# Queries turned in the score banks, key stacks in halves, and three convolution chunks dealt out in parts

## Chip, cores and metric

The kernel runs on one core of a Trainium2 chip. The metric is the device time of one execution in microseconds (us); lower is better. The core's engines run side by side, each working off its own instructions in order, and wait for each other through semaphores: PE (matrix products, results in PSUM banks), ACT (activations, copies), DVE (elementwise work, reductions), POOL (elementwise work in SBUF) and SP (which issues the DMAs).

## The reference

Two layers over 16 learned meta tokens and a sequence of 1024, 1024 features wide. Each layer has a sliding-window attention with 16 heads of 64 on 2 key heads, and an mLSTM with 4 heads:

```python
def hybrid_layer(x, ...):
    h = rms_norm(x, norm_g)
    z = h @ w_in
    aq, ak, av, ag, mq, mk, mv, mi, mf, mo, mgate = jnp.split(z, split_points(), axis=-1)
    q = apply_partial_rope(rms_norm(aq.reshape(B, L, 16, 64), q_norm_g), cos, sin)
    k = apply_partial_rope(rms_norm(ak.reshape(B, L, 2, 64), k_norm_g), cos, sin)
    ya = sliding_window_sink_attention(q, k, v, sink).reshape(B, L, ATT_WIDTH) * jax.nn.silu(ag)
    qk = jax.nn.silu(causal_depthwise_conv(jnp.concatenate([mq, mk], axis=-1), conv_w, conv_b))
    hm = mlstm_chunkwise(mq, mk, mv, log_i, log_f)          # mq, mk: the halves of qk
    ym = rms_norm(hm) * jax.nn.sigmoid(mo) * jax.nn.silu(mgate)
    return x + jnp.concatenate([ya, ym], axis=-1) @ w_out
```

## The kernel before

All matrix products are made of float32r pieces: an operand is split into a high part (a copy to float32r, mostly on ACT) and a low part (what is left, a subtraction on DVE or POOL), and three products are added up in PSUM. Such pairs of a high and a low part are called stacks below.

A layer (`l` is 0 for the first, 1 for the second) goes through keys and values, attention, mLSTM and the output projection. During attention PE has two streams of work, written out by hand and kept in that order (`pin`, `in_order`):

- The foreground list `fg`: projections, cut into parts of some 6 to 9 matmuls by `projT_parts` and `projN_parts`. A projection collects in one bank of the pool `pj`, which has two; when it is complete, `done` evacuates it. Even blocks `j` project the gates (`g_tasks`, evacuated at L640), odd ones the next queries (`q_tasks`), block 7 the mLSTM's values (`v_parts`).
- The background list: for each pair of heads `j` (8 of them) and each tile `b` of 128 queries (9 in the first layer, 8 in the second) four steps. `s1` makes the scores of two heads in a bank pair `S` (L667, alternating between two tiles `SS`) and the softmax from them: masks, a reduction (L685), two exponentials (L688), a reciprocal and two scalings (L693). `s2`, two steps later, transposes the probabilities into the bank `T` (L704, L707) and splits them (L711 to L715). `s3` and `s4`, another step later, multiply by the values in the bank `O` (L731, L743), which L746 and L748 evacuate. `T` and `O` have one bank each.

`weave` deals the background out between the foreground parts. Extra work hangs on foreground parts by number (`at`): among it `q_stacks(j, g)`, which takes a `pj` bank, transposes four tiles of rotated queries X into it (L617), and writes the query stack with two copies (L600, L601) and two subtractions (L602, L603) of 64x512. `g` is the half: tiles 1 to 4 or 5 to 8. X is complete after the rotation on DVE, whose last write is L556. In the first layer the 16 meta queries are turned in a corner of an `O` bank (`QM`), evacuated by the same L600 to L603 at 64x16.

Heads 8 to 15 need the second key head, so the key stacks `Ks` are rewritten between `j` = 3 and 4: `k_stacks(1, g, i)` four times, each a copy (L436) and a subtraction (L437) of 64x576. The scheduler may order everything that is not on PE, and does so by its own simulation.

At the end of attention the first three steps' worth of blocks are still to drain ("tail"); `cv` holds the six chunks (two projections by three ranges of tokens, 272, 384 and 384 wide) of the first mLSTM head's convolution (`conv_tasks`). Two of them stand between the draining steps as whole projections of 24 matmuls (L186), each followed by its copy, four multiply-adds, a tanh and a last product. Then the banks `S`, `T`, `O` are given up for others, `in_order` ends, and `gates` follows with the remaining chunks.

Of the kernel before, what the change touches and what calls it, by code (L numbers as in the profile page):

```python
# [14 lines left out]
AF = mybir.ActivationFunctionType  # L15
ALU = mybir.AluOpType
# [19 lines left out]
EARLY = 80  # L36
FIRST = ((0, 0), (0, 1), (1, 0))
# [26 lines left out]
def build(ctx, tc, I, O):  # L64
# [4 lines left out]
    def pin(ins):  # L69

        return tc.keep_in_program_order(ins) if in_order[0] else ins
# [293 lines left out]
    for l in range(DEPTH):  # L365
# [64 lines left out]
        def k_stacks(kv, g, i):  # L430

            s0 = 64 * kv
            src = KT[s0:s0 + 64, 4 * g:4 * g + 4].rearrange("p a c -> p (a c)")
            d = 64 - s0 if i else s0
            hi, lo = [T[d:d + 64, 576 * g:576 * g + 576] for T in Ks]
            sc.activation(hi, src, AF.Copy)  # L436
            ve.tensor_tensor(lo, src, Ks[0][s0:s0 + 64, 576 * g:576 * g + 576], op=ALU.subtract)  # L437
# [181 lines left out]

        def q_meta_turn(j, ps):  # L620
            c0 = 128 * (j % 2)
            pin(pe.transpose(ps, A[j]["q"]["XM"][:, c0:c0 + 128], ident[:16, :16]))
# [30 lines left out]
        def att_tasks(j, st):  # L653
# [3 lines left out]
            def s1(b):  # L657
                t0, p = TT[b]
                S = SS[blk[0] % 2]
                blk[0] += 1  # L660
                k0, kn, o = (0, 16, 128) if b == 0 else (0, 144, 128) if b == 1 else (16 + (b - 2) * 144, 272, 0)
                for h in range(2):
                    U = st["Q", b > 4]
                    i = (b - 1) % 4
                    lq = U[:, 1024 + 16 * h:1040 + 16 * h] if b == 0 else U[:, 512 * h + 128 * i:512 * h + 128 * i + 128]
                    for i in range(2):
                        pin(pe.matmul(S[:p, h, o + 2 - 2 * h:o + 2 - 2 * h + kn], lq, Ks[i][:, k0:k0 + kn],  # L667
                                  start=(i == 0), stop=(i == 1)))
                if st.setdefault("S", 0) < 2:
                    ve.tensor_copy(cols(S, 1, 783, 1), snk[:, l, 2 * j:2 * j + 2].rearrange("p (h c) -> p h c", c=1))  # L670
# [20 lines left out]
                for h in range(2):  # L691
                    Pn = P[:p, 1 + 144 * h:145 + 144 * h]
                    sc.activation(Pn, Pn, AF.Copy, scale=mx[:p, 2, h:h + 1])  # L693
                live[b] = P
# [154 lines left out]
        def conv_tasks(h, wgf, st):  # L849
            def chunk_task(which, c):  # L850
# [8 lines left out]
                ps = projT(wgf(), 128 * which, t0, n)  # L859
# [10 lines left out]
            return [lambda w=w, c=c: chunk_task(w, c) for w in range(2) for c in range(3)]  # L870
# [172 lines left out]
        for j in range(8):  # L1043
# [11 lines left out]
        at = {n0 + 6: [lambda: k_turn(0), lambda: (k_stacks(0, 0, 0), k_stacks(0, 0, 1)), lambda: v_stacks(0, 0)],  # L1055
              n0 + 15: [lambda: k_turn(1), lambda: (k_stacks(0, 1, 0), k_stacks(0, 1, 1)), lambda: v_stacks(0, 1)],
# [10 lines left out]
        ns = len(steps) // 8  # L1067

        def step(i):

            out = [lambda: None] * (2 * (i < 3) + (i < 2))
            if i < len(steps):
                j, b, s1 = steps[i][:3]
                out.append(lambda: s1(b))
                if (j, b) in ((3, 6), (3, 7), (4, 1), (4, 2)):
                    out.append(lambda: k_stacks(1, j - 3, b - 6 if j == 3 else b - 1))
# [12 lines left out]
        for j in range(8):  # L1089
# [16 lines left out]
            if j == 7:  # L1106
                at.setdefault(10, []).append(lambda: q_stacks(7, 1))
            else:
                at.setdefault((9 if j else 8) + extra, []).append(lambda j=j: q_stacks(j, 1))
                at.setdefault(21 + extra if j % 2 else 20, []).append(lambda j=j: q_stacks(j + 1, 0))  # L1110
# [8 lines left out]
        cv = conv_tasks(0, wc[0], M[0])  # L1119
        weave(cv[:2], step(8 * ns) + step(8 * ns + 1) + step(8 * ns + 2))  # L1120
# [3 lines left out]
        for f in cv[2:]:  # L1124
            f()
# [181 lines left out]
```

## Time and profile before

| | us |
|---|---|
| median of 3 runs | 1950.03 (1949.86 to 1952.85) |
| the profiled execution, its time | 1953.92 |
| its span, first to last instruction | 1952.2 |
| PE busy | 1908.1 (98%) |
| DVE, ACT, POOL busy | 1088.3, 1067.7, 906.4 |
| attention of the first layer | about 78 to 395 of the span, its tail to 412 |
| attention of the second layer | about 1068 to 1358, its tail to 1376 |

Rows of the profile name a line of the kernel, the engine, the operation, and the tiles it writes and reads. In rows in order of time the first number is the start in us from the span's start, the second how long it took; what stands in brackets is how long the engine idled before it and what ended that. In the list of waits stand the total, the number of waits and the longest.

### The profile page before, as it was taken

What the parts mean: (1) busy time and instruction counts of PE and PEld (TensorE: products, weight loads), DVE (VectorE), ACT (ScalarE), POOL (GpSimd) and SP (SyncE); (2) the same over time, 40 slices, a digit from 0 to 9 for tenths busy, and PEclk for the clock granted to TensorE, in tenths of its full rate; (3) what the DMA queues carried; (4) which work ended last, traced back from release to release, by engine and by line L of the source; (5) the groups of instructions that cost most, each with busy time, mean ns of one, the idle gap of its engine ahead of it and who ended that gap; (6) DMA issues with size and microseconds to landing.
All of it is one profiled execution on the core that took longest, in us unless ns stands there. A gap on an engine that the chain in (4) does not pass through costs nothing.

```text
span 1952.2 us, 36164 instructions
## 1 busy us (share of the span) xinstructions
PE 1908.1 (98%) x12827; PEld 1799.7 (92%) x12827; DVE 1088.3 (56%) x2966; ACT 1067.7 (55%) x3133; POOL 906.4 (46%) x1102
## 2 busy tenths in 40 slices
PE   8999999999999999999999999999999999999999
PEld 7998898999999999977789999999999999998887
DVE  7777777667454363532445678776673635437211
ACT  6577776747454544643334777776464535446221
POOL 3544544336545454564325345444365444547332
PEclk9999999999999999999999999999999999999999
DMA  4111111121222121455541111112122121226543
GB/s 153 44 37 49 39 43 35 37 65 35 62 60 58 41 56 55 146 164 168 176 132 50 39 37 54 43 36 59 39 58 64 40 67 50 57 62 187 171 149 121
DMA packets 150838, 148.28 MB, mean 76 GB/s; under 512 B 15081, under 2 KB 123921, under 8 KB 150658
## 3 DMA queue, kind: packets, MB, share of 16 engines
q1 hardware_dynamic: 150658, 145.97, 25.5%
q8 instruction: 101, 1.65, 0.4%
q14 instruction: 79, 0.65, 0.1%
HBM read 122.58 MB, written 23.29 MB: 75 GB/s over the span
## 4 chain that ended last, share of the span: by engine, by line
PE 80%; DVE 6%; ACT 4%; issue 3%; POOL 3%; DMA 3%; SPq 0%; POOLq 0%; DVEq 0%; ACTq 0%
PE pj L186 35%; PE pj L226 13%; PE pss L1204 6%; PE pj L1204 6%; PE po L1204 5%; PE po L917 2%; PE S L667 2%; PE pss L917 2%; DMA raw<-in_w_in_dram 2%; PE O L743 2%; POOL RING L160 1%; PE O L731 1%; PE pt L917 1%; ACT t L688 1%; PE T L707 1%
## 5 line engine op out<-in xcount | busy, mean ns | idle before, releaser
L186 PE MATMUL pj<-H,RING 128*128 128x384 f32 (+2 forms) x3456 | 583.0, 322 | 0.0
L186 PEld LDWEIGHTS pj<-H,RING 128*128 128x128 f32 x3456 | 543.3, 188 | 2.5 <-issue 0.2
L160 POOL TENSOR_TENSOR RING<-raw,RING 128x512 fp32r<-128x512 f32 (+1 forms) x192 | 255.5, 1338 | 121.5 <-ACT RING L159 114.4
L226 PE MATMUL pj<-RING,H 128*128 128x256 f32 (+1 forms) x1920 | 268.3, 286 | 3.5 <-DVE u L640 3.5
L226 PEld LDWEIGHTS pj<-RING,H 128*128 128x128 f32 x1920 | 242.5, 189 | 4.0 <-DVE u L640 3.8
L226 PE MATMUL pj<-H,RING 128*128 128x384 f32 (+2 forms) x1152 | 215.0, 326 | 3.9 <-DVE u L603 3.9
L186 PE MATMUL pj<-RING,H 128*128 128x256 f32 x1536 | 209.9, 287 | 3.3 <-DVE H L300 1.6
L178 POOL TENSOR_TENSOR RING<-raw,RING 128x512 fp32r<-128x512 f32 x96 | 125.9, 1318 | 175.8 <-ACT RING L177 167.3
L186 PEld LDWEIGHTS pj<-RING,H 128*128 128x128 f32 x1536 | 193.8, 191 | 6.1 <-DVE H L300 2.1
L226 PEld LDWEIGHTS pj<-H,RING 128*128 128x128 f32 x1152 | 179.4, 189 | 4.8 <-PE T L707 2.3
L177 ACT ACTIVATE RING<-raw 128x512 fp32r<-128x512 f32 x128 | 80.7, 631 | 173.0 <-DMA raw<-in_w_out_dram 139.6
L159 ACT ACTIVATE RING<-raw 128x512 fp32r<-128x512 f32 (+1 forms) x196 | 122.8, 630 | 66.1 <-DMA raw<-in_w_in_dram 50.4
L752 POOL TENSOR_TENSOR u<-u,w1k 128x128 f32<-128x128 f32 (+1 forms) x136 | 63.7, 468 | 172.7 <-DVE w1k L748 168.6
L688 ACT ACTIVATE t<-S,mx 128x145 f32<-128x145 f32 (+1 forms) x272 | 100.3, 373 | 59.8 <-DVE mx L685 52.7
L718 POOL TENSOR_SCALAR_AFFINE_SELECT p<-p 128x512 fp32r<-128x512 f32 x112 | 72.4, 646 | 126.9 <-DVE p L714 126.4
L930 POOL TENSOR_TENSOR p<-u,p 128x258 fp32r<-128x258 f32 x64 | 49.7, 777 | 170.8 <-ACT p L929 155.6
L1204 PE MATMUL pss<-RING,H 128*128 128x512 f32 x384 | 120.5, 394 | 0.0
L1204 PE MATMUL pj<-RING,H 128*128 128x512 f32 x352 | 110.7, 396 | 0.0
L693 ACT ACTIVATE t<-t,mx 128x144 f32<-128x144 f32 (+1 forms) x272 | 97.5, 407 | 20.3 <-DVE mx L690 20.1
L866 DVE SCALAR_TENSOR_TENSOR t<-u,cw,t 128x384 f32<-128x384 f32 (+1 forms) x144 | 107.2, 744 | 2.2
L886 DVE SCALAR_TENSOR_TENSOR t<-t,pj 128x384 f32<-128x384 f32 (+2 forms) x48 | 24.5, 511 | 124.8 <-ACT t L885 124.7
L748 DVE TENSOR_TENSOR w1k<-O,w1k 64x128 f32<-64x128 f32 (+1 forms) x272 | 74.6, 274 | 34.2 <-ACT w1k L746 31.3
(344 smaller groups left out, 3804.6 us busy)
## 6 DMA issues: line engine op xcount, KB each, us to landing
raw<-in_w_out_dram SPq DMA_DIRECT2D x128, 256.0 KB, 2.8
raw<-in_w_in_dram SPq DMA_DIRECT2D x100, 256.0 KB, 2.8
raw<-in_w_in_dram SPq DMA_DIRECT2D x192, 128.0 KB, 2.3
spool<-u SPq DMA_DIRECT2D x56, 192.0 KB, 1.9
p<-x SPq DMA_DIRECT2D x24, 256.0 KB, 3.6
t<-spool SPq DMA_DIRECT2D x30, 192.0 KB, 3.4
p<-spool SPq DMA_DIRECT2D x26, 192.0 KB, 4.2
u<-em SPq DMA_DIRECT2D x8, 576.0 KB, 6.5
```

Source lines behind the costliest of these rows:

```text
L159: sc.activation(hi, raw[:, :, 0:o], AF.Copy)
L160: eng.tensor_tensor(lo, raw[:, :, 0:o], hi, op=ALU.subtract)
L177: sc.activation(hi, raw, AF.Copy)
L178: (ve if i > 8 and i % 2 else gp).tensor_tensor(lo, raw, hi, op=ALU.subtract)
L186: last = pin(pe.matmul(out, a, b, start=(i == 0), stop=(i == n - 1)))
L226: pin(pe.matmul(out(), x, y, start=(k + i == 0), stop=(k == n - 1 and i == 2)))
L688: sc.activation(P[:p, 145 * h:145 * h + 145], S[:p, h, 1 + 127 * h:146 + 127 * h], AF.Exp, bias=mx[:p, 0, h:h + 1], accum_out=mx[:p, 1, h: ...
L693: sc.activation(Pn, Pn, AF.Copy, scale=mx[:p, 2, h:h + 1])
L748: ve.tensor_tensor(y[64 * h:64 * h + 64, :p], O[0:64, p * h:p * h + p], up[0:64, p * h:p * h + p], op=ALU.add)
L866: ve.scalar_tensor_tensor(z, RAW[:, t0 + i:t0 + i + n], wcol(i), z, ALU.mult, ALU.add)
L917: pin(f(*a, **k))
L1204: pin(pe.matmul(ps[:p, :], a, b, start=(i + n == 0), stop=(i == 15 and n == len(terms) - 1)))
```

## The change

A query stack gets no bank of its own. The scores of a tile fill columns 1 to 274 or so of each of the two banks of `S`; `visits` gives each second step or so a visit: right behind the score matmuls of `s1`, `q_turn` transposes two query tiles into columns 384 to 511 of the two banks, and at the end of `s1` `q_take` writes them to the query stack, with two copies and two subtractions of 64x256. There are two visits for a former `q_stacks`, 30 in each layer, and each lies two steps ahead of the block that first needs it. The very first stack of a layer stays as it was.

`k_stacks` now takes a start and a number of tiles, and `KEYS` spreads the second key head over eight steps, two tiles each time.

`conv_tasks` can give its first chunks in parts, as the foreground lists do; the first three chunks are now 3, 4 and 4 parts, dealt out over the draining steps.

```diff
+KEYS = {(3, 6): (0, 2, 0), (3, 7): (0, 2, 1), (3, 8): (2, 2, 0), (4, 1): (2, 2, 1),
+        (4, 2): (4, 2, 0), (4, 3): (4, 2, 1), (4, 4): (6, 2, 0), (4, 5): (6, 2, 1)}
...
-        def k_stacks(kv, g, i):
+        def k_stacks(kv, a, n, i):
...
-            hi, lo = [T[d:d + 64, 576 * g:576 * g + 576] for T in Ks]
+            hi, lo = [T[d:d + 64, 144 * a:144 * a + 144 * n] for T in Ks]
...
+        def q_turn(S, j, g, i):
+
+            c0 = 128 * (j % 2)
+            X = A[j]["q"]["X", g == 1]
+            for k in range(2):
+                pin(pe.transpose(S[:, k, 384:512], X[:, 256 * (i + k) + c0:256 * (i + k) + c0 + 128], ident))
+
+        def q_take(S, j, g, i):
+
+            Q = q_unit(j, g)[:, 0:1024].rearrange("p (h a c) -> p h a c", h=2, a=4)[:, :, i:i + 2]
+            src = S[:, :, 384:512]
+            sc.activation(Q[0:64, 0], src[0:64], AF.Copy)
+            sc.activation(Q[64:128, 1], src[64:128], AF.Copy)
+            ve.tensor_tensor(Q[64:128, 0], src[0:64], Q[0:64, 0], op=ALU.subtract)
+            ve.tensor_tensor(Q[0:64, 1], src[64:128], Q[64:128, 1], op=ALU.subtract)
...
+                if visit:
+                    q_turn(S, *visit)
...
+                if visit:
+                    q_take(S, *visit)
...
+            every = [(w, c) for w in range(2) for c in range(3)]
+            first = [x for w, c in every[:parted]
+                     for x in projT_parts(wgf, 128 * w, *CH[c][:2], lambda ps, w=w, c=c: finish(w, c, ps))]
+            return first + [lambda w=w, c=c: whole(w, c) for w, c in every[parted:]]
...
+        visits = {j * ns + 4 * g + i + 1 - first_q - 2: (j, g, i)
+                  for j in range(8) for g in range(2) for i in (0, 2) if j + g > 0}
...
-                if (j, b) in ((3, 6), (3, 7), (4, 1), (4, 2)):
-                    out.append(lambda: k_stacks(1, j - 3, b - 6 if j == 3 else b - 1))
+                k = KEYS.get((j, b))
+                if k:
+                    out.append(lambda: k_stacks(1, *k))
...
-            if j == 7:
-                at.setdefault(10, []).append(lambda: q_stacks(7, 1))
-            else:
-                at.setdefault((9 if j else 8) + extra, []).append(lambda j=j: q_stacks(j, 1))
-                at.setdefault(21 + extra if j % 2 else 20, []).append(lambda j=j: q_stacks(j + 1, 0))
...
-        cv = conv_tasks(0, wc[0], M[0])
-        weave(cv[:2], step(8 * ns) + step(8 * ns + 1) + step(8 * ns + 2))
+        cv = conv_tasks(0, wc[0], M[0], 3)
+        nt = len(cv) - 3
+        weave(cv[:nt], step(8 * ns) + step(8 * ns + 1) + step(8 * ns + 2))
...
-        for f in cv[2:]:
+        for f in cv[nt:]:
             f()
```

What that does to the engines' orders is seen at three places. Rows name line, operation, output, inputs and shape; "x9" is nine alike in a row, and what a row waits for stands in brackets. Lines of the changed kernel are higher: L686 are the scores (before L667), L627 `q_turn`, L635 and L636 `q_take`, L439 the key subtraction, L727 and L730 the transposes into `T`, L754 and L766 the products into `O`, L228 projection parts.

PE in the second layer, `j` = 3, around the turn for the first half of `j` = 4. Before:

```order
L743 MATMUL O<-ptm_106,VM 128x128 x2
L743 MATMUL O<-p_15103,u 128x256 [waits Pool_49]
L743 MATMUL O<-p_15103,u 128x256
L617 MATMUL pj<-cst,u 128x128 x4
L226 MATMUL pj<-RING,H 128x256 x6
L667 MATMUL S_13188<-u 128x272 x4
L704 MATMUL T<-cst,t 32x128 [waits DVE_49,PE_49]
```

After:

```order
L686 MATMUL S_13240<-u 128x272 x4
L627 MATMUL S_13240<-cst,u 128x128 [waits DVE_49]
L627 MATMUL S_13240<-cst,u 128x128
L228 MATMUL pj<-RING,H 128x256 x6
L727 MATMUL T<-cst,t 32x128 [waits PE_49,Activation_49]
L730 MATMUL T<-cst,t 128x128 x2
```

Four transposes into `pj` became twice two behind a tile's scores, one step further ahead, and the first of these two waits for DVE.

DVE in the first layer, end of `j` = 3 and start of `j` = 4, between one block's evacuation of `O` and the next one's. Before:

```order
L748 TENSOR_TENSOR w1k<-O,w1k 64x128
L681 COPY_PREDICATED S_1046<-mask,S_1046 128x2x128 [waits PE_49]
L685 TENSOR_REDUCE mx<-S_1046 128x2 [waits DVE_49]
L602 TENSOR_TENSOR u<-pj,u 64x512 [waits Activation_49]
L603 TENSOR_TENSOR u<-pj,u 64x512
L437 TENSOR_TENSOR u<-u 64x576 [waits Activation_49]
L437 TENSOR_TENSOR u<-u 64x576
L690 RECIPROCAL mx<-mx 128x2 [waits Activation_49]
L670 COPY S_1045<-snk 128x2 [waits PE_49]
L714 TENSOR_TENSOR p_3308<-T,p_3308 128x256 [waits Activation_49]
L715 TENSOR_TENSOR ptm_106<-T,ptm_106 32x128
```

After:

```order
L771 TENSOR_TENSOR w1k<-O,w1k 64x128
L702 COPY_PREDICATED S_1046<-mask,S_1046 128x2x128 [waits PE_49]
L439 TENSOR_TENSOR u<-u 64x288 [waits Activation_49]
L439 TENSOR_TENSOR u<-u 64x288
L706 TENSOR_REDUCE mx<-S_1046 128x2 [waits DVE_49]
L711 RECIPROCAL mx<-mx 128x2 [waits Activation_49]
L737 TENSOR_TENSOR p_3328<-T,p_3328 128x256 [waits PE_49,Activation_49]
L738 TENSOR_TENSOR ptm_106<-T,ptm_106 32x128
L635 TENSOR_TENSOR u<-S_1046,u 64x256 [waits Activation_49]
L636 TENSOR_TENSOR u<-S_1046,u 64x256
L691 COPY S_1045<-snk 128x2 [waits PE_49]
```

The query's subtractions are half as wide and behind the split of `T`'s results (L737, L738) instead of ahead of it, and the key subtractions are half as wide.

PE in the first layer's tail. Before:

```order
L186 MATMUL pj<-H,RING 128x272 x24
L704 MATMUL T<-cst,t 32x128 [waits DVE_49,PE_49]
L707 MATMUL T<-cst,t 128x128 x2
L731 MATMUL O<-p_5660,u 128x256 [waits DVE_49,Activation_49]
L731 MATMUL O<-p_5660,u 128x256
L743 MATMUL O<-ptm_106,VM 128x128 x2
L743 MATMUL O<-p_5665,u 128x256 [waits Pool_49]
L743 MATMUL O<-p_5665,u 128x256
L704 MATMUL T<-cst,t 32x128 [waits DVE_49,PE_49]
L707 MATMUL T<-cst,t 128x128 x2
L186 MATMUL pj<-H,RING 128x384 x24
```

After:

```order
L730 MATMUL T<-cst,t 128x128 x2
L228 MATMUL pj<-H,RING 128x272 x9
L754 MATMUL O<-p_5713,u 128x256 [waits DVE_49,Activation_49]
L754 MATMUL O<-p_5713,u 128x256
L228 MATMUL pj<-H,RING 128x384 x12
L766 MATMUL O<-ptm_106,VM 128x128 x2
L766 MATMUL O<-p_5718,u 128x256 [waits Pool_49]
L766 MATMUL O<-p_5718,u 128x256
L228 MATMUL pj<-H,RING 128x384 x6
L727 MATMUL T<-cst,t 32x128 [waits DVE_49,PE_49]
L730 MATMUL T<-cst,t 128x128 x2
```

Projection parts of 9, 12 and 6 matmuls lie between two uses of `T`, where before there was none.

More of the change, by code (lines that the diff above doesn't have):

```diff
@@ L428, in k_turn @@
             sc.activation(KT[:, 4 * g:4 * g + 4, 16:144], ps[:, 0:512].rearrange("p (a c) -> p a c", a=4), AF.Copy)
-        def k_stacks(kv, g, i):
+        def k_stacks(kv, a, n, i):
             s0 = 64 * kv
-            src = KT[s0:s0 + 64, 4 * g:4 * g + 4].rearrange("p a c -> p (a c)")
+            src = KT[s0:s0 + 64, a:a + n].rearrange("p a c -> p (a c)")
             d = 64 - s0 if i else s0
-            hi, lo = [T[d:d + 64, 576 * g:576 * g + 576] for T in Ks]
+            hi, lo = [T[d:d + 64, 144 * a:144 * a + 144 * n] for T in Ks]
             sc.activation(hi, src, AF.Copy)
-            ve.tensor_tensor(lo, src, Ks[0][s0:s0 + 64, 576 * g:576 * g + 576], op=ALU.subtract)
+            ve.tensor_tensor(lo, src, Ks[0][s0:s0 + 64, 144 * a:144 * a + 144 * n], op=ALU.subtract)
         def v_stacks(kv, g):
@@ L659, in s1 @@
                 S = SS[blk[0] % 2]
+                visit = visits.get(blk[0])
                 blk[0] += 1
@@ L847, in v_parts, with conv_tasks, whole, finish @@
             return [x for t in range(9) for x in projN_parts(wgf, [t], 264, lambda ps, t=t: finish(t, ps))]
-        def conv_tasks(h, wgf, st):
-            def chunk_task(which, c):
+        def conv_tasks(h, wgf, st, parted=0):
+            def whole(which, c):
+                t0, n, _ = CH[c]
+                finish(which, c, projT(wgf(), 128 * which, t0, n))
+            def finish(which, c, ps):
                 tj = which * 4 + h
@@ L858, in chunk_task @@
                 t0, n, _ = CH[c]
-                ps = projT(wgf(), 128 * which, t0, n)
                 with tc.high_priority(offset=EARLY):
@@ L869, in chunk_task @@
                 ve.scalar_tensor_tensor(out[:, t0:t0 + n], th, 1.0, z, ALU.add, ALU.mult)
-            return [lambda w=w, c=c: chunk_task(w, c) for w in range(2) for c in range(3)]
+            every = [(w, c) for w in range(2) for c in range(3)]
+            first = [x for w, c in every[:parted]
+                     for x in projT_parts(wgf, 128 * w, *CH[c][:2], lambda ps, w=w, c=c: finish(w, c, ps))]
+            return first + [lambda w=w, c=c: whole(w, c) for w, c in every[parted:]]
         def mo_tasks(u, wgf, st, held=None):
@@ L1054, in build @@
         n0 = len(fq) - 24
-        at = {n0 + 6: [lambda: k_turn(0), lambda: (k_stacks(0, 0, 0), k_stacks(0, 0, 1)), lambda: v_stacks(0, 0)],
-              n0 + 15: [lambda: k_turn(1), lambda: (k_stacks(0, 1, 0), k_stacks(0, 1, 1)), lambda: v_stacks(0, 1)],
+        at = {n0 + 6: [lambda: k_turn(0), lambda: (k_stacks(0, 0, 4, 0), k_stacks(0, 0, 4, 1)), lambda: v_stacks(0, 0)],
+              n0 + 15: [lambda: k_turn(1), lambda: (k_stacks(0, 4, 4, 0), k_stacks(0, 4, 4, 1)), lambda: v_stacks(0, 1)],
               n0 + 21: [lambda: q_stacks(0, 0, "pss")] + ([lambda: q_meta(0, bank("po")[:, 0:16])] if first_q == 0 else [])}
```

## The prediction

> **What bounds the kernel.** I read the page's busy times first, then the chain that ended last, then the waits of PE, then busy time by stage.
>
> ```profile
> span 1952.2 us, 36164 instructions
> PE 1908.1 (98%) x12827; PEld 1799.7 (92%) x12827; DVE 1088.3 (56%) x2966; ACT 1067.7 (55%) x3133; POOL 906.4 (46%) x1102
> PE 80%; DVE 6%; ACT 4%; issue 3%; POOL 3%; DMA 3%; SPq 0%; POOLq 0%; DVEq 0%; ACTq 0%
> ```
>
> PE is the bound: 98% busy, and 80% of the chain. The change leaves PE's instruction count as it was (120 query transposes per pair of layers become the same 120 elsewhere), so all that it can win is idle PE time: 1952.2 - 1908.1 = 44.1 us. The stages tell where that lies (columns: stretch, length, busy us of PE, PEld, DVE, ACT, POOL, granted clock, DMA share, GB/s):
>
> ```profile
> 78.00:395.00 317.00, 301.21 (x2301) 292.21 (x2300) 228.90 (x686) 229.79 (x779) 137.66 (x191) 0.99 0.14 40
> 395.00:412.00 17.00, 15.77 (x110) 15.57 (x109) 10.96 (x29) 7.33 (x21) 7.46 (x11) 1.00 0.26 72
> 412.00:1068.00 656.00, 652.19 (x4100) 601.58 (x4099) 317.66 (x830) 310.63 (x833) 316.40 (x369) 1.00 0.31 91
> 1068.00:1358.00 290.00, 282.27 (x2186) 278.22 (x2185) 209.25 (x606) 210.04 (x690) 127.62 (x165) 1.00 0.16 43
> 1358.00:1376.00 18.00, 16.28 (x115) 16.08 (x114) 11.69 (x28) 7.62 (x23) 7.68 (x11) 1.00 0.26 70
> ```
>
> Attention of the first layer has 317 - 301.2 = 15.8 us of idle PE, of the second 7.7; the two tails, where the last blocks drain, 1.2 and 1.7. That is 26.4 us, the ceiling. The list of what PE waited for says which waits these are:
>
> ```profile
> PE O L731 <- DVE w1k L748: 6.4, 9, 1.7
> PE T L704 <- DVE ptm L715: 5.5, 5, 1.7
> PE pj L226 <- DVE u L603: 3.9, 5, 1.1
> PE pj L226 <- DVE u L640: 3.5, 3, 1.3
> PE O L731 <- DVE u L603: 2.8, 5, 1.1
> PE pj L617 <- DVE u L640: 2.2, 2, 2.0
> PE pj L210 <- DVE u L603: 0.5, 1, 0.5
> ```
>
> **Part one: queries no longer turned in a projection bank.** Each `q_stacks` took one of the two `pj` banks and gave it back after two copies and two subtractions, so the projection after next waited for L603. Those waits, 3.9 and 0.5, end, since no query uses `pj` any more: 4.4 us. The converse, the turning that waited for a bank (L617, 2.2), ends too, but 2.0 of it sits at the ramp of the second layer, and a `T` wait follows:
>
> ```profile
> 1077.27 0.66 PE L617 MATMUL pj<-cst,u 128*128 128x128 f32 x4 [1.96 <-DVE u L640]
> 1082.24 0.27 PE L704 MATMUL T<-cst,t 128*32 128x128 f32 x1 [1.37 <-DVE ptm L715]
> ```
>
> Without the first wait PE arrives at `T` earlier, while the softmax of that block is no earlier. Of these 3.3 us I take 2.0, between 0.6 and 3.3; with the other 0.2, this part gives 4.4 + 2.2 = 6.6. The `O` wait on L603 (2.8) is the meta query, which the change doesn't touch, and L640 (3.5) comes from two short projections in a row at a group's end: I cost both at nothing.
>
> The four evacuations become eight of half the width. Their price from the 512-wide and the 16-wide rows:
>
> ```profile
> L603 DVE TENSOR_TENSOR u<-pj,u x30: 693/693/694, 89.4 to 1339.1; 64x512 fp32r<-64x512 f32 x30
> L603 DVE TENSOR_TENSOR u<-O,u x7: 176/176/180, 104.8 to 349.6; 64x16 fp32r<-64x16 f32 x7
> L600 ACT ACTIVATE u<-pj x30: 570/592/594, 87.5 to 1337.2; 64x512 fp32r<-64x512 f32 x30
> L600 ACT ACTIVATE u<-O x7: 161/177/178, 104.2 to 349.0; 64x16 fp32r<-64x16 f32 x7
> ```
>
> DVE: (693 - 176) / 496 = 1.04 ns a column, 426 ns at 256; ACT 378. A stack costs DVE 4 x 426 - 2 x 693 = 318 ns more, ACT 328; for 30 stacks 9.5 and 9.8, 19.3 us in all, beside PE. Bounds: nothing where covered, 19.3 if never. PE idled for 23.5 of these 607 us, 4%, which is the share at which I charge it: -0.8.
>
> **Part two: key stacks in halves.** One place pays for bursts on DVE, the boundary of blocks 3 and 4 in the first layer:
>
> ```profile
> 231.89 0.68 DVE L602 TENSOR_TENSOR u<-pj,u 64x512 fp32r<-64x512 f32 x1 [0.28 <-ACT u L601]
> 232.59 0.69 DVE L603 TENSOR_TENSOR u<-pj,u 64x512 fp32r<-64x512 f32 x1
> 233.31 1.96 DVE L437 TENSOR_TENSOR u<-u 64x576 fp32r<-64x576 f32 x2
> 236.77 0.27 PE L704 MATMUL T<-cst,t 128*32 128x128 f32 x1 [0.88 <-DVE ptm L715]
> 238.95 0.57 PE L731 MATMUL O<-p,u 128*128 128x256 f32 x2 [1.69 <-DVE w1k L748]
> 230.00:240.00 10.00, 7.43 (x60) 6.99 (x59) 8.70 (x20) 9.79 (x28) 6.60 (x8) 0.96 0.20 53
> 240.00:250.00 10.00, 10.00 (x60) 9.64 (x60) 7.19 (x24) 5.22 (x19) 5.97 (x9) 0.87 0.26 75
> ```
>
> The burst is 0.68 + 0.69 + 1.96 = 3.3 us. After, half a query (2 x 0.43) and one pair of half key stacks (half of 1.96) stand there, 1.8. The 1.5 us less come off the 2.57 of waiting; the rest of the key work goes to neighbouring steps, whose rows show no wait. After the waits the granted clock fell to 0.96 and 0.87: 0.04 x 10 + 0.13 x 10 = 1.7 us more. The Trainium skill, "TensorE: Matmul & The Clock Gate", Part 1, puts the drop after an idle window of about 3.4 us; by it these two waits should have cost no clock, and the clock term would be 0 where the rows give up to 1.7. Whether the unprofiled runs had the drop isn't shown, so it stands only in the range.
>
> Two smaller waits stand right behind a query's evacuation:
>
> ```profile
> 152.34 0.47 PE L731 MATMUL O<-p,u 128*128 128x256 f32 x2 [0.69 <-DVE w1k L748]
> 214.54 0.47 PE L731 MATMUL O<-p,u 128*128 128x256 f32 x2 [0.45 <-DVE w1k L748]
> ```
>
> With 0.85 us of DVE work ahead of them instead of 1.38, I take 0.5 of the 1.1.
>
> **Part three: convolution in parts.** In each tail two blocks' transposes stand with no projection between, so the second waits for `T`:
>
> ```profile
> 400.90 0.27 PE L704 MATMUL T<-cst,t 128*32 128x128 f32 x1 [1.23 <-DVE ptm L715]
> 1364.96 0.27 PE L704 MATMUL T<-cst,t 128*32 128x128 f32 x1 [1.72 <-DVE ptm L715]
> 1365.20 4.45 PE L186 MATMUL pj<-H,RING 128*128 128x384 f32 x24
> ```
>
> In the changed order 27 projection matmuls lie between these transposes, some 4.5 us by the last row, where the wait they replace is 1.7 at most. Both waits go: 2.9. It can't be more: the third chunk was a filler there already, and its arithmetic on DVE and ACT is the same. What covers the gates' chain behind is the next projections, as now. On SP a few weight loads change places with stores of finished blocks; none of PE's waits above is on a load.
>
> **What is new on PE.** A visit's two transposes stand behind `s1` in the same bank, and need the rotated query X. In the second layer visits fall on steps 0, 2, 4, 6 instead of beside the projections' parts 9 and 21, the first of them a step or so earlier, and seven of the 30 now carry a DVE wait. Two of the tightest places (a visit would start where L667 ends, X is ready where L556 ends):
>
> ```profile
> 1200.37 0.67 PE L667 MATMUL S<-u 128*128 128x272 f32 x4
> 1200.99 0.42 DVE L556 TENSOR_TENSOR u<-u,t 128x256 f32<-128x256 f32 x1
> 1221.18 0.66 PE L667 MATMUL S<-u 128*128 128x272 f32 x4
> 1221.94 0.42 DVE L556 TENSOR_TENSOR u<-u,t 128x256 f32<-128x256 f32 x1
> ```
>
> X ends at 1201.41 and 1222.36, 0.4 and 0.5 us after L667. So these two wait about half a microsecond even as things stand; the DVE work of the visit before (0.85) can come on top. For seven I take 0.43 each, -3.0; bounds 0.9 (two places) and 7 x 1.35 = 9.5. Behind a waiting transpose stand the next projection and `T`, so a wait goes to the end in full.
>
> The second new tie is the bank. `s1` two steps later needs the query and the bank:
>
> ```profile
> 1156.88 0.66 PE L667 MATMUL S<-u 128*128 128x272 f32 x4
> 1161.04 0.71 ACT L693 ACTIVATE t<-t,mx 128x144 f32<-128x144 f32 x2
> 1166.24 0.66 PE L667 MATMUL S<-u 128*128 128x272 f32 x4
> ```
>
> From the end of `s1` (1157.54) the softmax takes until 1161.75; two copies (0.76) and two subtractions (0.85) make it 1163.4 at the latest, 2.9 us ahead of its user. I cost it at nothing. The Trainium skill, "PSUM — Partial Sum Buffer", on bank collisions, has it that two engines must not touch one bank and quadrant at once, even in other columns. By that rule the mask copy of a visited block waits for the transposes as well; no row of this profile shows it, and by the 2.9 us it changes nothing.
>
> **Sum.** 6.6 + 1.5 + 0.5 + 2.9 = 11.5 won, 0.8 + 3.0 lost: 7.7 us. The profiled execution took 1953.92 with its span of 1952.2, and the median of the runs is 1950.03, 3.9 lower; 1953.9 goes to 1946.2, and the median to 1942.3. I say 1942.
>
> **Rivals.** *Waits move* (chance 0.20): ACT and DVE, at 72% in these stages, set the pace, and what `pj` no longer holds is waited for at `T` and `O`; the first wait at 1077 with its follower is such a case. For: 14.7 us of PE's waits are on `T` and `O` already. Against: those are 19 waits in 136 steps. Then only the tails' 2.9 stay: 1947 to 1951. *The score bank holds PE up* (0.12, the slower side): `s1` two steps after a visit waits for `q_take`'s last subtraction. It decides once that comes over 2.9 us later than I put it; 60 visits with 0.3 us each are 18 us, against 11.5 won: 1956. Against it: ACT and DVE idle more than a quarter of the time, and a query delayed in one step has the next. *All waits of attention go* (0.06): 26.4 less a few, plus the clock: 1930 or so. The forecast has 0.62.
>
> Range 1934 to 1952: below, all of the 3.3, the 2.57, the clock's 1.7, the 1.1 and the smallest loss, 4.6 + 3.3 + 2.57 + 1.7 + 1.1 + 2.9 - 0.9 = 15.3, rounded up to 16; above, the moved waits with the X waits at part of their bound. This kernel's times can tell 0.2%, 3.9 us, from no change: faster 0.68 (forecast and all waits gone), same 0.20, slower 0.12.
>
> **What would show it.** Right: no PE wait at a projection for a query's subtraction, no `T` wait in the tails, waits around 237 under 1.2 us, and up to seven waits of the second layer's visits on the rotation. Wrong: `S` waiting for the query's subtractions step after step, or `T` and `O` waits above 20 us; then the cover that I read off ACT and DVE was not there.

## The result, and the profile after

The changed kernel is slower. It took 1955.34 us (median of 20 runs, 1951.6 to 1963.1), the kernel before 1952.68 (20 runs, the three known before among them). One run of the kernel before, at 2533 us, was a slow one and does not enter the ratio, which is 1.0024 (95% interval 1.0015 to 1.0032), some 4.7 us; the medians are 2.7 apart, the means without that run 4.5. A later repeat gave 1.0026 (1.0016 to 1.0036). The prediction was 1942 and "faster", against a median of 1950.03 in the three runs known then.

The page of the changed kernel, the execution that took 1953.47:

```profile
span 1951.7 us, 36265 instructions
PE 1905.6 (98%) x12827; PEld 1798.8 (92%) x12827; DVE 1099.5 (56%) x3034; ACT 1073.9 (55%) x3201; POOL 912.7 (47%) x1102
PE 76%; DVE 8%; ACT 5%; issue 4%; POOL 4%; DMA 3%; SPq 0%; POOLq 0%; DVEq 0%; ACTq 0%
```

DVE has 11 us more work, and 8% of the chain where it had 6%. The stages again (columns as before):

```profile
78.00:395.00 317.00, 299.75 (x2302) 291.30 (x2302) 232.91 (x720) 233.96 (x813) 138.94 (x191) 1.00 0.14 40
395.00:412.00 17.00, 17.00 (x121) 16.90 (x120) 10.49 (x26) 6.78 (x20) 7.30 (x11) 1.00 0.27 73
1068.00:1358.00 290.00, 280.30 (x2154) 276.71 (x2153) 217.00 (x638) 209.63 (x718) 124.45 (x162) 0.99 0.15 42
1358.00:1376.00 18.00, 18.00 (x133) 17.89 (x132) 10.84 (x28) 8.26 (x24) 9.46 (x13) 1.00 0.25 71
```

Both tails are full, as forecast. But PE idles 17.3 us in the attention of the first layer (15.8 before), and 9.7 in the second (7.7). What it waits for has changed:

```profile
PE O L754 <- DVE S L691: 8.2, 4, 3.6
PE O L754 <- DVE w1k L771: 6.8, 9, 1.4
PE O L754 <- ACT t L714: 3.1, 1, 3.1
PE O L754 <- DVE u L848: 2.1, 1, 2.1
PE O L754 <- ACT ptm L735: 1.8, 2, 1.2
PE pj L228 <- DVE u L658: 0.8, 2, 0.5
```

(The lines moved: L754 is the first `O` product, once L731; L771 evacuates `O`, once L748; L658 was L640.) The waits of projections for a query's subtraction are gone, and no visit (L627) waits for the rotation. In their place `O` is waited for, 22 us in these five rows where it was 10, and four waits are longer than any in attention before. That is one of the two signs that the prediction named for being wrong, `T` and `O` waits above 20 us.

A sharper measure than PE's idle time is the length of attention, from the start of the first score matmul of a layer to the start of the last: 313.3 us before and 313.1 after in the first layer, 286.9 and 291.1 in the second. Since each step's scores can be set against the same step of the other kernel, it shows where the time goes: the second layer won 3.6 us in block 0 and lost 4.6 between steps 1 and 2 of block 2, and 4.6 again in block 6; between and behind these it won 1.4 more in small pieces, which leaves the 4.2. This is the first of the two places, DVE, GpSimd and PE in the timeline of the changed kernel:

```profile
1134.33 0.56 DVE L771 TENSOR_TENSOR w1k<-O,w1k 64x128 f32<-64x128 f32 x2
...
1135.85 1.77 DVE L543 TENSOR_TENSOR u<-u,ssq__14119 128x512 f32<-128x512 f32 x1
...
1138.38 1.59 DVE L553 TENSOR_TENSOR t<-u,qrt 128x128 f32<-128x128 f32 x2
1140.01 0.42 DVE L635 TENSOR_TENSOR u<-S,u 64x256 fp32r<-64x256 f32 x1
1140.44 0.43 DVE L636 TENSOR_TENSOR u<-S,u 64x256 fp32r<-64x256 f32 x1
1140.90 0.42 DVE L658 SCALAR_TENSOR_TENSOR u<-t,pj 128x256 f32<-128x256 f32 x1
1141.23 0.42 DVE L557 TENSOR_TENSOR u<-u,qrt 128x256 f32<-128x256 f32 x1
1141.57 0.57 DVE L771 TENSOR_TENSOR w1k<-O,w1k 64x128 f32<-64x128 f32 x2
...
1135.78 1.29 POOL L162 TENSOR_TENSOR RING<-raw,RING 128x512 fp32r<-128x512 f32 x1
1137.90 1.28 POOL L162 TENSOR_TENSOR RING<-raw,RING 128x512 fp32r<-128x512 f32 x1
...
1138.58 0.38 PE L730 MATMUL T<-cst,t 128*128 128x128 f32 x2
1142.29 0.77 PE L754 MATMUL O<-p,u 128*128 128x256 f32 x2 [3.33 <-DVE S L691]
```

`O` has one bank. From 1138.96 PE waits for DVE to read it (L771), and DVE, working in order, first does the rotation of the late queries (L553, L557), a visit's two subtractions (L635, L636) and a gate's evacuation (L658). ACT had made its copy of `O` at 1138.06. The row names L691, the little copy behind L771 at 1142.07, because it came last. In the kernel before DVE's order at this place was the other way round, `O` (L748) ahead of the rotation (L551):

```profile
1144.44 0.57 DVE L748 TENSOR_TENSOR w1k<-O,w1k 64x128 f32<-64x128 f32 x2
1145.04 1.02 DVE L551 TENSOR_TENSOR t<-u,qrt 128x128 f32<-128x128 f32 x2
```

and PE waited 0.24 us. The wait also cost clock. These are the busy times and the granted clock (0.83) of two windows of 10 us, which hold the last 2.3 and 2.4 us of the two waits and what follows:

```profile
1140.00:1150.00 10.00, 7.71 (x41) 7.73 (x42) 7.09 (x21) 3.85 (x15) 1.55 (x3) 0.83 0.10 27
1290.00:1300.00 10.00, 7.58 (x40) 7.59 (x41) 7.06 (x20) 4.95 (x19) 1.55 (x3) 0.83 0.12 32
```

So 3.3 us of waiting became 4.6 us of delay. The clock's share can be read from two profiles further down, in which one of these two waits was not followed by a drop (granted clock 1.00 over the next 10 us): block 6 in `hold` and block 2 in `more6` lost 3.1 us there.

### The profile page after: what moved, and what is told of

Same layout as the page of the kernel before. It is cut to its first block, busy times and chain, and to the rows that moved or that the text cites. A ratio compares the mean times of both kernels' runs of the same rounds, so it can differ in the third digit from the quotient of the medians.

```text
span 1951.7 us, 36265 instructions
## 1 busy us (share of the span) xinstructions
PE 1905.6 (98%) x12827; PEld 1798.8 (92%) x12827; DVE 1099.5 (56%) x3034; ACT 1073.9 (55%) x3201; POOL 912.7 (47%) x1102
## 4 chain that ended last, share of the span: by engine, by line
PE 76%; DVE 8%; ACT 5%; issue 4%; POOL 4%; DMA 3%; SPq 0%; POOLq 0%; DVEq 0%; ACTq 0%
PE pj L188 31%; PE pj L228 15%; PE pss L1233 6%; PE pj L1233 6%; PE po L1233 5%; PE S L686 2%; PE po L947 2%; PE O L766 2%; PE pss L947 2%; DMA raw<-in_w_in_dram 1%; POOL RING L162 1%; PE O L754 1%; DVE t L893 1%; PE pt L947 1%; ACT t L709 1%
## 5 line engine op out<-in xcount | busy, mean ns | idle before, releaser
L162 POOL TENSOR_TENSOR RING<-raw,RING 128x512 fp32r<-128x512 f32 (+1 forms) x192 | 258.1, 1350 | 108.3 <-ACT RING L161 103.1
L228 PE MATMUL pj<-RING,H 128*128 128x256 f32 (+1 forms) x1920 | 268.6, 286 | 0.8 <-DVE u L658 0.8
L228 PEld LDWEIGHTS pj<-RING,H 128*128 128x128 f32 x1920 | 242.3, 189 | 1.2 <-DVE u L658 1.0
L228 PE MATMUL pj<-H,RING 128*128 128x384 f32 (+2 forms) x1296 | 241.9, 327 | 0.0
L228 PEld LDWEIGHTS pj<-H,RING 128*128 128x128 f32 x1296 | 202.6, 190 | 0.0
L775 POOL TENSOR_TENSOR u<-u,w1k 128x128 f32<-128x128 f32 (+1 forms) x136 | 66.2, 487 | 210.6 <-DVE w1k L771 198.3
L714 ACT ACTIVATE t<-t,mx 128x144 f32<-128x144 f32 (+1 forms) x272 | 98.1, 407 | 10.2 <-DVE mx L711 9.3
L1233 PE MATMUL po<-RING,H 128*128 128x512 f32 x288 | 91.4, 398 | 0.0
```

Of the source, the lines that this page charges most:

```text
L162: eng.tensor_tensor(lo, raw[:, :, 0:o], hi, op=ALU.subtract)
L228: pin(pe.matmul(out(), x, y, start=(k + i == 0), stop=(k == n - 1 and i == 2)))
L1233: pin(pe.matmul(ps[:p, :], a, b, start=(i + n == 0), stop=(i == 15 and n == len(terms) - 1)))
```

## The experiments

Theory 1: what counts is the place in the in-order queues of DVE and ACT. Theory 2: the load of ACT and DVE sets the pace, and a wait taken away anywhere comes back elsewhere. Theory 3: GpSimd's work slows DVE at the critical spot. All ratios are against the kernel before, run on the same chip. Its medians there were 1954.6 to 1955.0 us, so a thousandth is 2 us.

### The three parts, one at a time

`conv_only`, the convolution in parts alone:

```diff
-        cv = conv_tasks(0, wc[0], M[0])
-        weave(cv[:2], step(8 * ns) + step(8 * ns + 1) + step(8 * ns + 2))
+        cv = conv_tasks(0, wc[0], M[0], 3)
+        nt = len(cv) - 3
+        weave(cv[:nt], step(8 * ns) + step(8 * ns + 1) + step(8 * ns + 2))
```

> The kernel before with the convolution's parts alone. Theory 1 (the loss sits in the order that DVE's work takes where the queries were moved) and theory 2 (any work that is moved at ACT and DVE only shifts the waits) agree that the two tails lose their waits on T, 2.9 us. By theory 1 nothing gives that back: 1.5 to 3 us less than the kernel before. By theory 2 the chunks' remainder waits behind the tail instead: within 1 us of before.

Measured: 0.9989 (0.9979 to 0.9998), -2.1 us. The tails have no idle PE (windows of this run):

```profile
395.00:412.00 17.00, 17.00 (x120) 16.90 (x119) 10.86 (x28) 6.80 (x19) 6.26 (x9) 1.00 0.22 59
1358.00:1376.00 18.00, 18.00 (x130) 17.90 (x128) 10.15 (x26) 7.82 (x24) 8.55 (x12) 1.00 0.26 70
```

1.23 and 1.72 us are won and nothing gives them back. This part does what the prediction said. (This profile's first layer, with the code and the waits of the kernel before at 237 and 239, is 1.3 us shorter: the granted clock from 240 to 250 was 1.00 here and 0.87 there.)

`keys_only`, the key stacks in halves alone:

```diff
+KEYS = {(3, 6): (0, 2, 0), (3, 7): (0, 2, 1), (3, 8): (2, 2, 0), (4, 1): (2, 2, 1), ...}
-                if (j, b) in ((3, 6), (3, 7), (4, 1), (4, 2)):
-                    out.append(lambda: k_stacks(1, j - 3, b - 6 if j == 3 else b - 1))
+                k = KEYS.get((j, b))
+                if k:
+                    out.append(lambda: k_stacks(1, *k))
```

> The kernel before with the key stacks in halves alone. Theory 1: the burst of 3.3 us at the boundary of blocks 3 and 4 of the first layer shrinks, the waits there go from 2.57 to under 1.2, and the time is 1 to 3 us less than before (the upper end with the clock). Theory 2: the same key work over eight steps meets other evacuations, the waits there still sum to 2 to 3 us, time within 1 us of before.

Measured: 1.0015 (1.0004 to 1.0025), 3 us slower; the first layer's attention is 316.0 us, 2.7 longer. Neither theory had foreseen a loss of this size. The timeline of ACT, DVE and PE in this run shows it:

```profile
227.11 0.38 ACT L748 ACTIVATE w1k<-O 64x256 f32<-64x256 f32 x1
227.52 0.91 ACT L438 ACTIVATE u<-u 64x288 fp32r<-64x288 f32 x2
...
229.72 0.17 ACT L602 ACTIVATE u<-O 64x16 fp32r<-64x16 f32 x1
229.90 0.18 ACT L603 ACTIVATE u<-O 64x16 fp32r<-64x16 f32 x1
...
231.03 0.18 DVE L605 TENSOR_TENSOR u<-O,u 64x16 fp32r<-64x16 f32 x1
...
231.35 0.48 PE L733 MATMUL O<-p,u 128*128 128x256 f32 x2 [3.29 <-ACT t L695]
```

The meta query sits in a corner of `O` at this step. Its two copies now stand on ACT behind the first half copies of the keys (L438), a `T` evacuation and a step's exponentials, and `O` stays held until the last subtraction behind them (L605 on DVE) ends at 231.21. The wait at 237 to 239 did shrink, to one of 1.25, but this one is new.

`queries_only`, the queries in the score banks alone (`visits`, `q_turn`, `q_take`; the calls of `q_stacks` in the foreground removed):

> The kernel before with the queries in the score banks' free columns alone. Both theories: this part carries the loss, 5 to 9 us more than before, since the tails gain 2.9 in the kernel after and it is still 3 to 5 slower. Theory 1: two waits of PE at O of over 3 us each, in the second layer, with DVE's evacuation of O behind rotation and query subtractions, as in the kernel after at 1142 and 1292; together with the clock behind them over half of the loss. Theory 2: waits on O of 0.5 to 1.5 us over both layers, and no two large ones.

Measured: 1.0040 (1.0026 to 1.0055), 7.8 us slower; attention 315.3 and 291.9 us. As theory 1 had it, the second layer has two waits on `O` with 6.9 us together and the longest 3.6. The first layer, 2 us longer, has fifteen waits on `O` of 0.2 to 2.8: theory 2 has something there.

### Which visits: a first guess that failed

`hold`: the late halves of even blocks keep a projection bank in the second layer.

```diff
-                  for j in range(8) for g in range(2) for i in (0, 2) if j + g > 0}
+                  for j in range(8) for g in range(2) for i in (0, 2) if j + g > 0
+                  and not (last and g == 1 and j % 2 == 0)}
...
+            if last and j % 2 == 0:
+                at.setdefault(9 if j else 8, []).append(lambda j=j: q_stacks(j, 1))
```

> The kernel after, but in the second layer the late halves of even blocks are turned in a projection bank of their own, as before; all else as in after. Theory 1: the two waits at 1142 and 1292 (3.3 and 3.6 us) and the clock of 0.83 behind them go, some 9 us, against 2 to 3 us of waits for the projection bank that come back: 5 to 8 us less than the kernel after, 1 to 4 less than the kernel before. Theory 2: the waits move on; within 2 us of the kernel after.

Measured: 1.0039 (1.0024 to 1.0054), no better; the second layer's attention is 294.6 us, 3.6 longer than in the kernel after. The large waits stayed (8.0 us, longest 3.6). The 3.6 us more are about what block 0 had won: with its late half back in `pj`, the waits of the start of the second layer are back (1.9 and 1.4). (A new wait of 1.1 at `pj` in block 4, and a clock that did not drop behind the second large wait, nearly cancel.) So the colliding visit is another. At step 0 of blocks 2, 4 and 6 a visit is made for the block's *early* half, tiles 3 and 4, and its subtractions meet the rotation of the late half, which hangs on the same block's first parts.

### That visit a step earlier

`after_again` is the changed kernel itself, beside the others.

> The kernel after once more, beside the three that follow on the same chip. Expected by every theory: 3 to 6 us more than the kernel before; waits of PE at O near 1142 and 1292 of 3.3 and 3.6 us again, since they come from the order of DVE's queue. If these two are gone in this profile, they were chance and theory 1 falls. The wait between the layers, near 930 to 945, on the rows of x that arrive by DMA, was 1.8 to 4.9 us in six kernels that don't differ there: it may come out anywhere between.

Measured: 1.0026 (1.0016 to 1.0036); attention 314.5 and 291.3; the two waits are there again (longest 3.6). They are no chance.

`early2`:

```diff
-        visits = {j * ns + 4 * g + i + 1 - first_q - 2: (j, g, i)
+        visits = {j * ns + 4 * g + i + 1 - first_q - 2 - (last and g == 0 and i == 2 and j % 2 == 0): (j, g, i)
```

> The kernel after, with one thing moved: in the second layer, the visit that fell on the first step of blocks 2, 4 and 6 is made one step earlier, so that its copies and subtractions no longer stand in DVE's queue between the rotation of the late queries and O's evacuation. Theory 1 (those 0.85 us of DVE, with the rotation moved ahead of O's evacuation, are the two large waits): the waits of 3.3 and 3.6 us fall under 1 us each, the second layer's attention gains 7 to 9 us against the kernel after, and the time is 5 to 9 us less. Theory 2 (load, whatever the order): O or T waits as much elsewhere; within 2 us of the kernel after. Theory 3 (GpSimd's work slows DVE there): the waits shrink by the 0.85 each, time 2 to 3 us less.

Measured: 1.0014 (1.0005 to 1.0024), 2.3 us less than the kernel after, though the intervals touch; second layer 289.6. Theory 1's 5 to 9 us did not come; the time fits theory 3's 2 to 3, the waits fit neither: they are 1.98 and 2.05 now, some 1.4 and 1.5 shorter, and one of 1.68 on `O` is new at 1217. The visit is out of the burst, but the rotation still stands ahead of `O` (DVE, POOL and PE of this run):

```profile
1143.92 2.03 DVE L553 TENSOR_TENSOR t<-u,qrt 128x128 f32<-128x128 f32 x2
1145.88 0.57 DVE L771 TENSOR_TENSOR w1k<-O,w1k 64x128 f32<-64x128 f32 x2
...
1143.89 1.27 POOL L162 TENSOR_TENSOR RING<-raw,RING 128x512 fp32r<-128x512 f32 x1
...
1146.60 0.47 PE L754 MATMUL O<-p,u 128*128 128x256 f32 x2 [1.98 <-DVE S L691]
```

`more6`, the next weights' splitting later in the even blocks of the second layer:

```diff
-            at = {i: [nxt.more] for i in (3, 8, 12, 17)}
+            at = {i: [nxt.more] for i in ((6, 10, 14, 18) if last and j % 2 == 0 else (3, 8, 12, 17))}
```

> The kernel after, with the splitting of the next weights (ACT and GpSimd) started three parts later in the even blocks of the second layer; the order of DVE's queue around the two waits is the same as in the kernel after. Theory 3: the scaling of the late queries goes from 1.77 us back to about 0.7, the rotation from 1.59 to about 1.0, the two waits shrink from 3.3 and 3.6 to under 2, and 4 to 6 us are won. Theory 1: DVE's queue has the same work ahead of O's evacuation; the waits shrink by at most the 1.1 to 1.6 us that GpSimd's overlap costs, and if that overlap just moves to other rows of the burst, not at all: 0 to 3 us less than the kernel after.

Measured: 1.0027 (1.0016 to 1.0038), the waits unchanged (3.33 and 3.58); the second layer, 290.0, is 1.1 shorter because the first of them kept its clock. It doesn't decide: GpSimd's L162 still lay over the scaling (1.76 us) and the rotation (1.60), since it follows when the weights land. How much of the 3.3 us is GpSimd's share stays open; the rows of the kernel after bound it. The scaling took 1.77 where it takes 0.69 elsewhere, the two rotation instructions 1.59 where they take 0.57 at 1120 (1.02 at this place in the kernel before): at most 2.1 us.

`nokeys_early2`: as `early2`, the key stacks left whole.

> The kernel after with the visits of the second layer moved as in the run before and the key stacks left whole, as in the kernel before. Theory 1: besides the two waits of the second layer, the wait of 3.07 us at the boundary of blocks 3 and 4 of the first layer (on ACT's copies of half key stacks) goes as well: 3 us less than with the visits moved alone, 3 to 6 us less than the kernel before. Theory 2: within 2 us of the kernel after.

Measured: 1.0006 (0.9995 to 1.0016); second layer 287.5. It is 3.9 us less than the kernel after, more than theory 2 allowed, and not less than the kernel before, as theory 1 had it. The 3.07 us at 229 went, but a wait of 2.72 came at 239, where the whole key subtractions (L437, 3.01 us for two) stand in DVE's queue, as they did in the kernel before (0.88 and 1.69 of waiting there): the first layer, 315.9, is no shorter than in `early2` (315.8). In that layer it came out as theory 2 said.

### The rotation behind `O`

`order2`: as `nokeys_early2`, and the late rotation written one part later in the second layer.

```diff
-                at.setdefault(1 + i, []).append(x)
+                at.setdefault(1 + i + (1 if last else 0), []).append(x)
```

> Queries in the score banks and the convolution in parts, key stacks whole, the visits of the second layer moved one step earlier as before, and in the second layer the rotation of the late queries written one part later; with that DVE's queue has O's evacuation ahead of the rotation, as in the kernel before. Theory 1: the two waits of 2.0 us that were left near 1146 and 1293 go, and visits that wait for the rotated queries come in their place (0.2 to 0.8 each); the second layer's attention gains about 3 us against the run with visits moved and whole key stacks, and 3 us in all: 1 to 4 us less than the kernel before. Theory 2 (the load of ACT and DVE sets the pace, whatever the order): as many microseconds of waits elsewhere in the second layer; within 1.5 us of the run with visits moved and whole key stacks.

Measured: 0.9977 (0.9966 to 0.9988), 4.5 us *less* than the kernel before; second layer 283.4 us, 7.7 less than in the kernel after with the same instructions but for the keys. DVE at the place, and PE (lines two lower here: L769 evacuates `O`, L551 rotates):

```profile
1141.18 0.57 DVE L769 TENSOR_TENSOR w1k<-O,w1k 64x128 f32<-64x128 f32 x2
...
1142.69 0.47 DVE L551 TENSOR_TENSOR t<-u,qrt 128x128 f32<-128x128 f32 x1
...
1141.90 0.48 PE L752 MATMUL O<-p,u 128*128 128x256 f32 x2
```

`O` is read first, and PE goes on without a wait. Of visits that wait for the rotation there are two, 0.78 and 1.06 us. Against `nokeys_early2`, which differs by this one move, the second layer is 4.0 us shorter. This settles the two large waits of the second layer for theory 1: with the evacuation ahead of the rotation they are gone, at the same load.

### Where the queries pay

`ramp`: the convolution in parts, and only the late half of block 0 and the early half of block 1, in the second layer, in the score banks.

```diff
+        inS = lambda j, g: last and j + g == 1
...
-                  for j in range(8) for g in range(2) for i in (0, 2) if j + g > 0}
+                  for j in range(8) for g in range(2) for i in (0, 2) if j + g > 0 and inS(j, g)}
```

> The kernel before with the convolution in parts, and with two query halves of the second layer alone turned in the score banks: the late half of block 0 and the early half of block 1. All other queries are turned in a projection bank, as before. Theory 1: the wait of 1.96 us for the projection bank at the start of the second layer's attention and the T wait of 1.37 behind it go and nothing comes in their place, as in the kernel after, where block 0 gained 3.6 us; with the convolution's 2 us this is 4 to 6 us less than the kernel before. Theory 2: the ramp's gain is waited for again within the next blocks; 1 to 3 us less than the kernel before.

Measured: 0.9967 (0.9954 to 0.9980), 6.5 us less; attention 313.4 and 284.6. Block 0 won 3.5 us, and all that is left of the two waits of 1.96 and 1.37 is one of 0.28 at `T`. But the second layer as a whole won 2.3: in block 2 PE waits 1.59 us for `O`, where it waited 0.24 in the kernel before (DVE, POOL and PE of this run):

```profile
1141.42 1.82 DVE L541 TENSOR_TENSOR u<-u,ssq__14063 128x512 f32<-128x512 f32 x1
...
1143.56 0.57 DVE L769 TENSOR_TENSOR w1k<-O,w1k 64x128 f32<-64x128 f32 x2
...
1140.16 2.53 POOL L160 TENSOR_TENSOR RING<-raw,RING 128x512 fp32r<-128x512 f32 x2
...
1144.27 0.47 PE L752 MATMUL O<-p,u 128*128 128x256 f32 x2 [1.59 <-DVE w1k L769]
```

`O` stands ahead of the rotation here, no visit is near, and the scaling took 1.82 us beside GpSimd's L160, where it took 0.69 in the kernel before. That is theory 3 without theory 1, 1.1 of the 1.59 us. A share of the waits of the kernel after is then likely GpSimd's too; how large it is stays open.

`first_layer`: the convolution in parts, and `inS` true in the first layer only.

> The kernel before with the convolution in parts, and the queries of the first layer alone turned in the score banks; key stacks whole. Theory 1 puts the loss of the queries on two places of the second layer; without these the first layer's pj waits (about 8 us) should turn to a gain. But in all profiles so far the first layer's attention came out 0 to 3 us longer with these queries, with O waits in place of the pj waits, which is theory 2 for this layer. By the first: 2 to 6 us less than the kernel before. By the second: from 1 us less (the convolution's 2 us with a loss of 1) to 2 us more.

Measured: 1.0003 (0.9993 to 1.0012); attention 314.9 and 287.2. The first layer's queries win nothing and lose 1.6 us. Its waits at `pj` turn into waits at `O`, as theory 2 had it. But one of these is a matter of place again. At the end of block 6, DVE and PE in the kernel before and then in this run (L603 is the last subtraction of the meta query, L735 the split of `T`):

```profile
349.61 0.18 DVE L603 TENSOR_TENSOR u<-O,u 64x16 fp32r<-64x16 f32 x1
...
349.93 0.47 PE L731 MATMUL O<-p,u 128*128 128x256 f32 x2 [0.29 <-DVE u L603]
```

```profile
352.28 0.42 DVE L735 TENSOR_TENSOR p<-T,p 128x256 fp32r<-128x256 f32 x1 [0.16 <-POOL u L773]
...
353.21 0.18 DVE L603 TENSOR_TENSOR u<-O,u 64x16 fp32r<-64x16 f32 x1
...
353.53 0.55 PE L752 MATMUL O<-p,u 128*128 128x256 f32 x2 [2.06 <-DVE u L846]
```

The meta query's copies and subtractions, which hold `O`, stood ahead of the split of `T` (then L714, at 350.62) and now stand behind it. All nine profiles with the first layer's queries in the score banks have this wait of 2.06, the six others 0.29. In this run the step took 8.5 us where it took 5.7: 2.9 us more, and the layer's whole loss is 1.6. No run puts that evacuation back, so whether load or order keeps the first layer from winning stays open.

`second_layer`: `inS` true in the second layer only, with `order2`'s two moves.

> The kernel before with the convolution in parts and the queries of the second layer alone turned in the score banks, with its visits and rotation placed as in the run order2; first layer as before, key stacks whole. Theory 1 (the place in DVE's queue decides, layer by layer): the first layer comes out as in the kernel before, the second gains 3 to 4 us as in order2: 4 to 7 us less than the kernel before, the same as ramp or up to 2 us better. Theory 2 (load decides): 1 to 3 us less than the kernel before.

Measured: 0.9969 (0.9959 to 0.9979), 1948.51 us against 1954.62; attention 312.9 and 283.7. The second layer's window of this run:

```profile
1068.00:1358.00 290.00, 285.20 (x2212) 281.31 (x2211) 215.07 (x643) 214.18 (x728) 128.90 (x166) 1.00 0.16 45
```

PE idles 4.8 us in this layer's attention, where it idled 9.7 in the kernel after; DVE was busy for 75% of it in both (212.0 of 283.7 us, 216.9 of 291.1). `ramp` and this one are the best versions here, and can't be told apart.

`keys_late`, which tests the place on ACT: the half key stacks alone, the first three entries a step later. The second layer has no step (4, 0), so one half copy and its subtraction are left out there, and only the first layer can be compared.

```diff
-KEYS = {(3, 6): (0, 2, 0), (3, 7): (0, 2, 1), (3, 8): (2, 2, 0), ...
+KEYS = {(3, 7): (0, 2, 0), (3, 8): (0, 2, 1), (4, 0): (2, 2, 0), ...
```

> The kernel with the key stacks in halves alone, but its first two pairs of halves written one step later, so that ACT's two small copies of the meta query stand ahead of the first half copies instead of behind them. If the loss of keys_only (3.29 us of waiting at 231.35 in its trace) is this place in ACT's queue, that wait falls below 1 us and the first layer's attention is 2 to 4 us shorter than in keys_only, 0 to 2 shorter than before; the time is within 2 us of the kernel before or less. If it is the load of smaller copies, waits of 3 us or so stay somewhere between 225 and 250 and the time stays 2 to 4 us above the kernel before.

Measured: 0.9993 (0.9984 to 1.0002); first layer 312.9 us, 3 less than `keys_only`. ACT and PE:

```profile
225.60 0.18 ACT L602 ACTIVATE u<-O 64x16 fp32r<-64x16 f32 x1
225.79 0.18 ACT L603 ACTIVATE u<-O 64x16 fp32r<-64x16 f32 x1
...
227.10 0.91 ACT L438 ACTIVATE u<-u 64x288 fp32r<-64x288 f32 x2
...
235.51 0.98 PE L228 MATMUL pj<-H,RING 128*128 128x272 f32 x6 [1.61 <-DVE u L605]
```

The 3.29 us wait is gone, one of 1.61 is left. The keys lost by their place, not by their size; and in the better place the halves win nothing that the spread of the profiles would show (312.9 us, against 312.0 to 313.4 in four with the first layer of the kernel before).

## Why the prediction was wrong

- **The tails, 2.9 won:** right; 2.95 us of idle PE went (1.23 and 1.72), and alone they measured 2.1 (0.4 to 4.1).
- **The start of the second layer, 2.0 of 3.3:** too small for block 0, which won 3.6 us in the kernel after and 3.5 in `ramp`; but `ramp` kept only 2.3 of it to the end of the layer.
- **The other queries, 4.4 + 0.2 won at `pj`:** the waits went, and the gain did not come. This is the first step that failed: I took a wait at `pj` off the sum without asking what PE meets next. In the second case of the prediction, "waits move", I had it right, with too small a chance, and for the first layer alone, where it was not load only (the wait of 2.06).
- **Extra evacuations, 0.8 lost at the 4% share:** the step that failed most. A share of idle time is no price for work in an in-order queue. The 0.85 us of a visit cost nothing at most steps, and stood in the two bursts that cost 4.6 us each. My list of what the visits touch had `S` and X; I never read what stands on DVE between two evacuations of `O`, nor that the scheduler would turn round rotation and evacuation. The order of the changed kernel could be read before any run; the three places that I read leave this one out. Why the scheduler turned them round was not tested.
- **Seven visits waiting for X, 3.0 lost:** wrong, none waited. The rotation now stands ahead of `O`'s evacuation, so X is there in time; the cost came up in another place, at three times the size (9.2). With the evacuation in front again, in `order2`, two visits do wait, 1.8 us together.
- **`S` at nothing:** right; its waits are 0.9 and 0.6, of which 0.6 stood there before.
- **Keys, 1.5 won:** wrong, 2.7 lost. I shortened the burst on DVE and didn't look at what the half copies stand ahead of on ACT. The waits around 237, forecast under 1.2, are 1.3 at 239 and 3.1 at 229.
- **Two waits behind a query's evacuation, 0.5 won:** not seen. They were 0.69 and 0.45; in the kernel after there are waits of 1.30 and 0.87 one step later each, at 155 and 217. (`keys_only` has the second as well, 0.84.)
- **Clock, only in the range, and only as a gain:** a wait of 3.3 us became 4.6 us of delay, so new long waits belonged in the sum with the clock behind them, as a loss.

By the profiles most of the change's loss is in the second layer: won 3.6 at its start, lost 9.2 at two places, 4.2 lost in all. In the first layer it loses some 1.4: five profiles with its first layer have 313.1 to 315.8 us (mean 314.3), four with that of the kernel before 312.0 to 313.4 (312.9). The measured time lies near the third case of the prediction, 1956, by luck: that was for `S` waiting on the query's subtractions, which did not happen.

## What to carry to other kernels

Work that moves off one bank goes into the same in-order queues of ACT and DVE: before counting a removed wait as won, list what then stands between two evacuations of the next single-buffered bank, burst by burst; an average load says nothing of it. Where a scheduler sets the order, read the new order at the tightest places before pricing the change, for a due date that moves earlier can put a long job ahead of a short one that another engine waits for. Here, in runs against the kernel before, a rotation written a part later and a visit made a step earlier, with the keys left whole, turned +0.24% into -0.23%; the convolution's part with the queries at the start of the second layer alone gave -0.33%.

## What the runs showed of the hardware

The clock after a wait is partly chance. In the kernel after and in `early2`, which has the same first layer, the same wait of 3.07 us on `O` ends at 229.1 and 229.8. PE's busy time, matmuls and granted clock in the 4 us from 230, first after, then `early2`:

```profile
230.00:234.00 4.00, 4.00 (x36) 1.00 0.01 2
```

```profile
230.00:234.00 4.00, 4.00 (x24) 0.62 0.00 0
```

One kept its clock, the other did a third less in the same time. And two waits of 2.0 us in `early2` were followed by 1.00 and by 0.83 over the next 10 us. The wait of 2.06 us at the end of block 6 says it most plainly, since nine profiles have it in the same place: over the next 4 us four granted 1.00 and the step took 7.0 us, five granted 0.57 to 0.59 and it took 8.5. Of the ten waits of 3.3 to 3.6 us in the five profiles that have both, eight were followed by a drop. The Trainium skill, "TensorE: Matmul & The Clock Gate", Part 1, speaks of a free-running window of about 3.4 us; that it runs free agrees with these rows, but the 0.83 after 2.0 us of waiting shows that the drop comes well below 3.4. The spread goes the same way: 20 runs of the kernel after reach over 11.5 us at mean clocks of 0.998 (1951.6) down to 0.993 (1960.6 and 1962.5), 8 of `order2` over 3.7 us at 0.997 to 0.999.

DVE waits for GpSimd. The scaling L543 began at 1135.85, just behind GpSimd's L162 (1135.78 for 1.29), and ended 0.55 us after that one's end; alone it takes 0.69, and it took 0.69 as well where a GpSimd instruction (L775) began 0.05 us behind it, at 1187.45. The Trainium skill, "SBUF — State Buffer", section "Who interferes with whom", says that a DVE instruction with two SBUF inputs contends with a GpSimd instruction that reads SBUF, and that the order of issue decides which of them is blocked; the rows agree.

The wait between the layers, for rows of x that come by DMA, was 1.8 us in the kernel after and 5.0 in its repeat. Single profiles of identical code thus differ by 3 us there, which is why the readings above use the length of attention and not the span.
